# Two recurrence units go from four accumulators to seven products, one attention unit goes the other way, and the first load, the last weights and the last sums are rearranged

## The chip, the core and the metric

The kernel runs on one core of a Trainium2 chip. The number is the device time of one launch in microseconds (us). TensorE (PE) multiplies, VectorE (DVE) and ScalarE (ACT) work on elements, GpSimd (POOL) does some element work, and SyncE (SP) issues nearly all transfers from memory.

## The reference

A hybrid trunk of two layers on 544 frames: 512 frames of a new stream and 32 of a running one. D_MODEL is 2048.

```python
def rec_layer(...):                        # layer 0
    proj = rms_norm(x, g) @ w_in           # 2048 -> 2048 + 2048 + 1024 + 1024
    xa, ga, xb, gb = split(proj)
    xa_c = causal_conv(xa, ...)            # width 4
    r, i = sigmoid(blocks of xa_c @ w_r + b_r), sigmoid(blocks of xa_c @ w_i + b_i)
    ya = scan(h = a_t * h + u_t)           # a, u from r, i, lam, xa_c
    yb = pool_mix(xb)                      # trailing means, per-group map, scale
    return x + concat(ya * silu(ga), yb * silu(gb)) @ w_out      # 3072 -> 2048

def att_layer(...):                        # layer 1
    q, k, v, gt = split(rms_norm(x, g) @ w_in)                   # 2048 -> 4 x 2048
    o = sb_attend(q, k, v)                 # 16 heads, stick-breaking: a suffix sum over the keys
    return x + (o * silu(gt)) @ w_out      # 2048 -> 2048
# rms_norm(., norm_final) of the end; keys, values and states are outputs too
```

## The kernel before

Activations lie as 128 features by 544 frames, in two halves of 272 frames (H1, H2). A product in full precision is three TensorE products of split numbers: `mm3` gives high weight times high activation (line 108), high weight times low activation (L109) and low weight times high activation (L110), 128x272 each. Weights come by SP's queue into `wraw` (line 195, 384 KB in a tile of 128x768, seven buffers) and are split by `wsplit`: ACT copies the high part `wh` (L203), DVE subtracts it to get `wl` (L204), three buffers each. Activations are split the same way (`xh`, L230, and `xl`, L231).

A *unit* multiplies 2 x 128 output features by 2048 inputs. Twelve of the sixteen input blocks lie as a 2x2 square of blocks B11, B12, B21, B22 (six times 128 inputs by one half of the frames each), the other four lie in `XP`. There are two forms:

- `plain_unit`: four accumulators, 64 triples, so 192 matmuls. It splits four 128x768 weight tiles and the `XP` tiles, and DVE takes each accumulator out with one multiplication (`scaled_out`, L449).
- `unit`: seven products of six triples and 16 triples for `XP`, so 58 triples, 174 matmuls. For it DVE makes four sums of weight tiles (L385, L389, L394, L400, 128x768), splits seven weight tiles instead of four, adds four products up (L408) and adds an addend to each of the four results (L447). It also needs four blocks T1 to T4, sums of the activation blocks, built once for a layer by `sums_by_pairs`: `loads` fetches, `makes` adds (L283 to L285) and splits, `lastload` and `three` make T4 (L299).

Layer 0 has 16 recurrence units n = 0 to 15 (all plain before), eight pool units (`unit`) and the output projection (eight units). The gates of unit n (`back`, 12 matmuls into `pg`) are called at hook 2 of unit n+1. A hook is a function called between two parts of a unit, so that other work stands among the unit's own. Layer 1 has 16 heads h with two units each: `ha` (queries and keys) and `hb` (values and gate). Before, ha of head 0 is plain, with the three parts of the sums in its hooks 1, 2 and 3, and all others are `unit`s. Behind the output projection comes a *last part* for the four `XP` blocks: for each half of the frames and each of 16 output blocks m it takes a 128x512 weight tile, four triples, an add to `x3` (L1187), a square and a sum of squares (L1193). The final norm follows: `rstd_sums` gives the sums of squares to TensorE (L137), and `finish` scales (L1172) and stores. The first half's 16 `finish` calls stand in the second half's loop at m >= 8.

Code stands in the order in which it is called, but a scheduler orders each engine's instructions; `high_priority` moves what is in it ahead of other work that is ready.

## Time and profile before

| | |
|---|---|
| median of 3 runs | 1927.06 us (1926.83 to 1929.6) |
| the profiled execution | 1924.38 us, span 1922.6 us |
| granted TensorE clock, mean | 0.996 of full speed (2.4 GHz) |
| PE busy | 1890.3 us (98%) |
| DVE busy | 1526.8 us (79%) |
| ACT busy | 935.0 us (49%) |
| POOL busy | 181.8 us (9%) |

The span runs from the first to the last instruction; 1.78 us of the profiled time lie around it. Busy shares are means over all stages.

### The profile page before, as it was taken

How to read it: one execution, taken by the hardware profiler on the slowest of the kernel's cores; microseconds unless marked ns; L12 is line 12 of the kernel's file. 1: busy time of each engine (PE TensorE's matmuls, PEld its weight loads, DVE VectorE, ACT ScalarE, POOL GpSimd, SP SyncE). 2: the span in 40 equal slices, each digit the busy share in tenths (PEclk: the TensorE clock that was granted, in tenths of full speed). 3: DMA queues.
4: the chain of work that ended last, by engine and by line, in shares of the span. 5: the costliest groups of instructions: out<-in, count | busy, mean ns of one | idle time of the engine just before them, and what ended most of it. 6: DMA issues, size and time to landing. Idle time of an engine off the chain costs nothing.

```text
span 1922.6 us, 37274 instructions
## 1 busy us (share of the span) xinstructions
PE 1890.3 (98%) x14872; PEld 1871.7 (97%) x14872; DVE 1526.8 (79%) x2487; ACT 935.0 (49%) x1313; POOL 181.8 (9%) x294
## 2 busy tenths in 40 slices
PE   8999999999999999999999999999999999999997
PEld 8999999999999999999899999999999999999997
DVE  8766687689888666567988888888888888897987
ACT  7766666665335433335544444444444444454443
POOL 0000012011010000000211111111111101110000
PEclk9999999999999999999999999999999999999998
DMA  6454443323337645458333333334333433385344
GB/s 223 118 151 132 127 150 122 101 84 117 106 108 240 205 142 165 138 157 247 109 97 104 120 101 110 104 117 128 92 106 117 120 94 106 106 273 177 124 128 150
DMA packets 133215, 260.37 MB, mean 135 GB/s; under 512 B 16113, under 2 KB 44017, under 8 KB 133041
## 3 DMA queue, kind: packets, MB, share of 16 engines
q1 hardware_dynamic: 131808, 256.59, 43.2%
q8 instruction: 117, 1.92, 0.4%
q10 hardware_dynamic: 1152, 1.11, 0.2%
q14 instruction: 58, 0.47, 0.1%
q0 software_dynamic: 80, 0.28, 0.0%
HBM read 220.98 MB, written 36.95 MB: 134 GB/s over the span
## 4 chain that ended last, share of the span: by engine, by line
PE 79%; DVE 12%; DMA 4%; issue 3%; ACT 1%; POOL 0%; SPq 0%; DVEq 0%; ACTq 0%; POOLq 0%
PE pp L108 24%; PE pp L110 24%; PE pp L109 24%; DVE wl L204 4%; DMA wraw<-in_w_in_att 2%; DVE big L907 1%; PE pm L109 1%; DMA T<-x2g 1%; PE pm L110 1%; PE pa L924 1%; PE pm L108 1%; PE pg L108 1%; DVE xl L231 1%; PE pg L109 1%; DMA wraw<-in_w_in_rec 1%
## 5 line engine op out<-in xcount | busy, mean ns | idle before, releaser
L108 PE MATMUL pp<-xh,wh 128*128 128x272 f32 x3156 | 912.7, 289 | 11.3 <-ACT wh L203 7.5
L110 PE MATMUL pp<-xh,wl 128*128 128x272 f32 x3156 | 909.3, 288 | 3.2 <-DVE wl L204 3.0
L109 PE MATMUL pp<-xl,wh 128*128 128x272 f32 x3156 | 907.0, 288 | 0.1
L203 ACT ACTIVATE wh<-wraw 128x768 fp32r<-128x768 f32 (+2 forms) x634 | 494.9, 783 | 771.5 <-PE pp L109 526.5
L204 DVE TENSOR_TENSOR wl<-wraw,wh 128x768 fp32r<-128x768 f32 (+2 forms) x634 | 553.9, 878 | 148.8 <-ACT wh L203 145.2
L108 PEld LDWEIGHTS pp<-xh,wh 128*128 128x128 f32 x3156 | 595.2, 189 | 13.6 <-ACT wh L203 8.1
L110 PEld LDWEIGHTS pp<-xh,wl 128*128 128x128 f32 x3156 | 593.9, 188 | 6.7 <-DVE wl L204 6.3
L109 PEld LDWEIGHTS pp<-xl,wh 128*128 128x128 f32 x3156 | 594.5, 188 | 0.8 <-DVE xl L231 0.3
L110 PE MATMUL pp<-xp,wl 128*128 128x272 f32 x1152 | 331.6, 288 | 0.0
L108 PE MATMUL pp<-xp,wh 128*128 128x272 f32 x1152 | 331.4, 288 | 0.0
L109 PE MATMUL pp<-xp,wh 128*128 128x272 f32 x1152 | 330.0, 286 | 0.0
L108 PEld LDWEIGHTS pp<-xp,wh 128*128 128x128 f32 x1152 | 217.3, 189 | 1.1 <-issue 1.1
L110 PEld LDWEIGHTS pp<-xp,wl 128*128 128x128 f32 x1152 | 216.6, 188 | 0.0
L109 PEld LDWEIGHTS pp<-xp,wh 128*128 128x128 f32 x1152 | 216.2, 188 | 0.0
L447 DVE TENSOR_TENSOR e<-pp,e 128x272 f32<-128x272 f32 x156 | 65.5, 438 | 42.2 <-PE pp L110 38.3
L408 DVE TENSOR_TENSOR e<-pp,e 128x272 f32<-128x272 f32 x200 | 82.0, 430 | 5.4 <-PE pp L110 4.7
L109 PE MATMUL pp<-T,wh 128*128 128x272 f32 x256 | 73.7, 288 | 0.0
L108 PE MATMUL pp<-T,wh 128*128 128x272 f32 x256 | 73.7, 288 | 0.0
L110 PE MATMUL pp<-T,wl 128*128 128x272 f32 x256 | 73.5, 287 | 0.0
L230 ACT ACTIVATE xh<-T 128x544 fp32r<-128x544 f32 x72 | 46.4, 655 | 47.7 <-DVE T L283 14.4
L385 DVE TENSOR_TENSOR wraw<-wraw,wraw 128x768 f32<-128x768 f32 x50 | 47.6, 952 | 22.6 <-DMA wraw<-in_w_in_att 8.1
L209 ACT ACTIVATE T<-T 128x544 fp32r<-128x544 f32 (+1 forms) x72 | 45.1, 645 | 35.9 <-DMA T<-in_cv 15.6
(254 smaller groups left out, 2115.4 us busy)
## 6 DMA issues: line engine op xcount, KB each, us to landing
wraw<-in_w_in_att SPq DMA_DIRECT2D x128, 384.0 KB, 3.3
wraw<-in_w_in_rec SPq DMA_DIRECT2D x96, 384.0 KB, 3.3
wraw<-in_w_out_rec SPq DMA_DIRECT2D x64, 384.0 KB, 3.6
wraw<-in_w_in_att SPq DMA_DIRECT2D x64, 256.0 KB, 3.2
wraw<-in_w_in_rec SPq DMA_DIRECT2D x48, 256.0 KB, 3.2
wraw<-in_w_out_att SPq DMA_DIRECT2D x32, 384.0 KB, 3.8
...
```

Of the source, the lines that this page charges most:

```text
L108: nc.tensor.matmul(out, wh, xh, start=start, stop=False)
L109: nc.tensor.matmul(out, wh, xl, start=False, stop=False)
L110: nc.tensor.matmul(out, wl, xh, start=False, stop=stop)
L203: nc.scalar.activation(hi, src, AF.Copy)
L204: nc.vector.tensor_tensor(lo, src, f(hi), ALU.subtract)
L209: nc.scalar.activation(a, src, AF.Copy)
L230: nc.scalar.activation(h, src, AF.Copy)
L231: nc.vector.tensor_tensor(l, src, f(h), ALU.subtract)
L385: nc.vector.tensor_tensor(w[1], w[0], w[1], ALU.subtract)
L408: nc.vector.tensor_tensor(sm[name], acc[p], sm[other], ALU.add)
L447: nc.vector.tensor_tensor(src, bk, addend, ALU.add)
L907: nc.vector.tensor_tensor_scan(inc[:, o:o + w][:, ::-1], s, s, 1.0, ALU.mult, ALU.min)
```

## The change

1. **Start.** The first weight tile comes in two transfers, 128x128 and 128x640, and is split in two.
2. **Recurrence.** The sums T1 to T4 of this layer are made over units 10 to 13 (loads at hook 4 of 10, 11, 12, makes at hook 0 of 11, 12, 13, T4 at hook 0 of 14), and units 14 and 15 become `unit`s.
3. **Attention.** hb of head 0 becomes plain; the sums' parts go to hb of head 0 (hooks 0 and 1) and ha of head 1 (hook 0).
4. **Last part.** The first half keeps its 16 split weight tiles in the space of the activation blocks, and the second half uses them again. The add to `x3` is given high priority, the first half's 16 `finish` calls are spread over m = 4 to 13, and its reciprocal roots come earlier (m = 1 and 3, before 2 and 6).

```diff
-    def wsplit(src):
+    def wsplit(src, cut=0):
...
-        nc.scalar.activation(hi, src, AF.Copy)
-        nc.vector.tensor_tensor(lo, src, f(hi), ALU.subtract)
+        for a, b in ((0, cut), (cut, n)):
+            if a < b:
+                nc.scalar.activation(hi[:, a:b, :], src[:, a:b, :], AF.Copy)
+                nc.vector.tensor_tensor(lo[:, a:b, :], src[:, a:b, :], f(hi[:, a:b, :]), ALU.subtract)
...
-        def chunk(m, c):
-            early.append(raw(w_in_rec[m, :, c * NS:min((c + 1) * NS, KT)]))
+        def chunk(m, c, cut=0):
+
+            src = w_in_rec[m, :, c * NS:min((c + 1) * NS, KT)]
+            if cut:
+                t = raw()
+                nc.sync.dma_start(t[:, :cut * P], flat(src[:, :cut]))
+                nc.sync.dma_start(t[:, cut * P:], flat(src[:, cut:]))
+            else:
+                t = raw(src)
+            early.append((t, cut))
...
-        chunk(0, 0)
+        chunk(0, 0, 1)
...
-        one, two, three = sums(xgd)
+        loads, makes, lastload, three = sums_by_pairs(xgd)
...
-            if n == 9:
-                with_hooks(hk, {4: [one]})
-            if n == 10:
-                with_hooks(hk, {4: [two]})
-            if n == NRB - 1:
-                with_hooks(hk, {3: [three]})
-            plain_unit(srcs[n], rg_out(c), hk)
+            if 10 <= n <= 12:
+                with_hooks(hk, {4: [loads[n - 10]]})
+            if 11 <= n <= 13:
+                with_hooks(hk, {0: [makes[n - 11]]})
+            if n == 13:
+                with_hooks(hk, {4: [lastload]})
+            if n == 14:
+                with_hooks(hk, {0: [three]})
+            (plain_unit if n < 14 else unit)(srcs[n], rg_out(c), hk)
...
                 with_hooks(ha, {0: [lambda: pend.append(rows(x2g))],
-                                1: [lambda: box.append(rstd_sums(rps, 0, N)), one, lambda: pend.pop()()],
-                                2: [two], 3: [three],
+                                1: [lambda: box.append(rstd_sums(rps, 0, N)), lambda: pend.pop()()],
                                 4: [spread_rbc]})
+                with_hooks(hb, {0: [one], 1: [two]})
...
+            if h == 1:
+                with_hooks(ha, {0: [three]})
...
-            unit((w_in_att[4 * h + 2], w_in_att[4 * h + 3]), att_out(c), hb, LAST if h == NH - 1 else ORDER)
+            if h:
+                unit((w_in_att[4 * h + 2], w_in_att[4 * h + 3]), att_out(c), hb, LAST if h == NH - 1 else ORDER)
+            else:
+                plain_unit((w_in_att[2], w_in_att[3]), att_out(c), hb)
...
+        def last_weights(m):
+            if m == len(kept):
+                if m % 3 == 0:
+                    sl = SLOT[ORDER[m // 3]]
+                    room[:] = [xs.tile([P, 3, 4, P], F32R, tag=f"{q}{sl}", name=nm("wlast")) for q in ("xh", "xl")]
+                with tc.high_priority():
+                    src = raw(w_out_att[m, :, 2 * NS:]).rearrange("p (a b) -> p a b", b=P)
+                    hi, lo = (r[:, m % 3] for r in room)
+                    nc.scalar.activation(hi, src, AF.Copy)
+                    nc.vector.tensor_tensor(lo, src, f(hi), ALU.subtract)
+                kept.append((hi, lo))
+            return kept[m]
...
-                if hf == 1 and m == 2:
+                if hf == 1 and m == 1:
...
-                if hf == 1 and m == 6:
-                    nc.scalar.activation(rbc[:, H1], rstd_spread(rps, rst), AF.Copy)
-                with tc.high_priority():
-                    hi, lo = wsplit(raw(w_out_att[m, :, 2 * NS:]))
+                if hf == 1 and m == 3:
+                    with tc.high_priority():
+                        nc.scalar.activation(rbc[:, H1], rstd_spread(rps, rst), AF.Copy)
+                hi, lo = last_weights(m)
...
-                nc.vector.tensor_tensor(x3[m][:, s], x3[m][:, s], ps, ALU.add)
+                with tc.high_priority():
+                    nc.vector.tensor_tensor(x3[m][:, s], x3[m][:, s], ps, ALU.add)
...
-                if hf == 1 and m >= 8:
-                    finish(2 * (m - 8), 0, rbc[:, H1])
-                    finish(2 * (m - 8) + 1, 0, rbc[:, H1])
+                if hf == 1 and 4 <= m < 14:
+                    for q in range(16 * (m - 4) // 10, 16 * (m - 3) // 10):
+                        finish(q, 0, rbc[:, H1])
```

Three places in the order of DVE's instructions. A line of after stands 2 lines later in the code than in before from line 204 on, later by more further down (L285 of after is L283 of before, L449 is L447, L451 is L449, L1221 is L1187, L1189 is L1172). The first place is where T4 is made (its subtractions write `T_`). Before, in plain unit 11 (the call stands in unit 15, the scheduler takes it as soon as its operands are there), with two weight splits (`wl`) among them:

```order
L299 TENSOR_TENSOR T_3549<-T_3549,xh_443_3518 128x544
L204 TENSOR_TENSOR wl_3767<-wraw_3764,wh_3766 128x768
L588 TENSOR_TENSOR big_3629<-ev_3622,big_3629 128x548
L299 TENSOR_TENSOR T_3549<-T_3549,xl_444_3519 128x544
L299 TENSOR_TENSOR T_3551<-T_3551,xh_443_3518 128x544
L299 TENSOR_TENSOR T_3553<-T_3553,xh_443_3518 128x544
L299 TENSOR_TENSOR T_3551<-T_3551,xl_444_3519 128x544
L299 TENSOR_TENSOR T_3553<-T_3553,xl_444_3519 128x544
L204 TENSOR_TENSOR wl_3809<-wraw_3806,wh_3808 128x768
```

After, in unit 14, which has become a `unit`:

```order
L206 TENSOR_TENSOR wl_4690<-wraw_4687,wh_4689 128x768
L301 TENSOR_TENSOR T_4434<-T_4434,xl_451_3591 128x544
L402 TENSOR_TENSOR wraw_4687<-wraw_4687,wraw_4563 128x768
L387 TENSOR_TENSOR wraw_4847<-wraw_4845,wraw_4847 128x768
L410 TENSOR_TENSOR e_4683<-pp_4664,e_4657 128x272
L410 TENSOR_TENSOR e_4588<-pp_4664,e_4588 128x272
L233 TENSOR_TENSOR xl_565_4518<-T_4434,xh_564_4517 128x544
L301 TENSOR_TENSOR T_4436<-T_4436,xh_450_3590 128x544
L206 TENSOR_TENSOR wl_4714<-wraw_4687,wh_4713 128x768
L206 TENSOR_TENSOR wl_4739<-wraw_4736,wh_4738 128x512
L391 TENSOR_TENSOR wraw_4877<-wraw_4849,wraw_4847 128x768
L206 TENSOR_TENSOR wl_4774<-wraw_4535,wh_4773 128x768
```

T4's subtractions (L299, now L301) and their splits (L233) stand now among weight sums (L402, L387, L391) and additions of products (L410) of the unit itself.

The second place is the first head of the attention. Before, where ha of head 0 ends, its accumulators `pp` are taken out into `T_` (L449) behind the sums of the activation blocks (L283 to L285) and their splits (`xl`, L231):

```order
L283 TENSOR_TENSOR T_10940<-T_10940,T_10936 128x544
L231 TENSOR_TENSOR xl_1543_11009<-T_10932,xh_1542_11008 128x544
L284 TENSOR_TENSOR T_10936<-T_10936,T_10938 128x544
L231 TENSOR_TENSOR xl_1545_11011<-T_10940,xh_1544_11010 128x544
L285 TENSOR_TENSOR T_10938<-T_10940,T_10938 128x544
L204 TENSOR_TENSOR wl_11234<-wraw_11226,wh_11233 128x768
L231 TENSOR_TENSOR xl_1543_11009<-T_10938,xh_1542_11008 128x544
L394 TENSOR_TENSOR wraw_11226<-wraw_11226,wraw_11259 128x768
L449 TENSOR_TENSOR T_11179<-pp_10859,rbc 128x272
L449 TENSOR_TENSOR T_11179<-pp_10860,rbc 128x272
L204 TENSOR_TENSOR wl_11262<-wraw_11259,wh_11261 128x768
L231 TENSOR_TENSOR xl_1541_11007<-T_10936,xh_1540_11006 128x544
```

After, at the same end of ha of head 0:

```order
L451 TENSOR_TENSOR T_11151<-pp_10902,rbc 128x272
L451 TENSOR_TENSOR T_11151<-pp_10903,rbc 128x272
L206 TENSOR_TENSOR wl_11305<-wraw_11302,wh_11304 128x768
L387 TENSOR_TENSOR wraw_11546<-wraw_11544,wraw_11546 128x768
L451 TENSOR_TENSOR T_11184<-pp_10904,rbc 128x272
L451 TENSOR_TENSOR T_11184<-pp_10905,rbc 128x272
L212 TENSOR_TENSOR T_11188<-T_11151,T_11187 128x544
L206 TENSOR_TENSOR wl_11347<-wraw_11344,wh_11346 128x768
L212 TENSOR_TENSOR T_11194<-T_11184,T_11193 128x544
L391 TENSOR_TENSOR wraw_11601<-wraw_11548,wraw_11546 128x768
L206 TENSOR_TENSOR wl_11420<-wraw_11417,wh_11419 128x768
L285 TENSOR_TENSOR T_11206<-T_11206,T_11202 128x544
```

The taking out (L451) now comes ahead of the first sum (L285), which stands in hb; one weight sum (L387) and one more (L391) of ha of head 1 stand between them.

The third place is the end of the last part's second half. Before, behind the last additions to `x3` (L1187), with `finish` multiplications (L1172) among them:

```order
L1187 TENSOR_TENSOR big_22480<-big_22480,pp_23509 128x272
L1172 SCALAR_TENSOR_TENSOR T_22093<-T_22093,vec,rbc 128x272
L1172 SCALAR_TENSOR_TENSOR T_22094<-T_22094,vec,rbc 128x272
L1193 TENSOR_TENSOR sqacc<-sqacc,e_23529 128x272
L1187 TENSOR_TENSOR big_22480<-big_22480,pp_23536 128x272
L1172 SCALAR_TENSOR_TENSOR big_22287<-big_22287,vec,rbc 128x272 x2
L1193 TENSOR_TENSOR sqacc<-sqacc,e_23556 128x272
L1187 TENSOR_TENSOR big_22681<-big_22681,pp_23563 128x272
L1172 SCALAR_TENSOR_TENSOR big_22480<-big_22480,vec,rbc 128x272 x2
L1187 TENSOR_TENSOR big_22681<-big_22681,pp_23589 128x272
L1172 SCALAR_TENSOR_TENSOR big_22681<-big_22681,vec,rbc 128x272 x2
L148 TENSOR_SCALAR rs_71<-pa_23615 128x3
```

After:

```order
L1221 TENSOR_TENSOR big_22310<-big_22310,pp_23408 128x272
L1189 SCALAR_TENSOR_TENSOR big_22704<-big_22704,vec,rbc 128x272 x2
L1221 TENSOR_TENSOR big_22310<-big_22310,pp_23429 128x272
L1227 TENSOR_TENSOR sqacc<-sqacc,e_23422 128x272
L1227 TENSOR_TENSOR sqacc<-sqacc,e_23443 128x272
L1221 TENSOR_TENSOR big_22503<-big_22503,pp_23448 128x272
L1227 TENSOR_TENSOR sqacc<-sqacc,e_23462 128x272
L1221 TENSOR_TENSOR big_22503<-big_22503,pp_23469 128x272
L1227 TENSOR_TENSOR sqacc<-sqacc,e_23483 128x272
L1221 TENSOR_TENSOR big_22704<-big_22704,pp_23490 128x272
L1221 TENSOR_TENSOR big_22704<-big_22704,pp_23506 128x272
L148 TENSOR_SCALAR rs_71<-pa_23522 128x3
```

The `finish` multiplications (L1189 now) are gone from the last six additions (L1221).

## Rows read from the trace of the kernel before

**Rows 1.** The page: the span, and busy time, share of the span and instructions of each engine.

```profile
span 1922.6 us, 37274 instructions
...
PE 1890.3 (98%) x14872; PEld 1871.7 (97%) x14872; DVE 1526.8 (79%) x2487; ACT 935.0 (49%) x1313; POOL 181.8 (9%) x294
```

**Rows 2.** Busy time by stretch, in one of the recurrence's last units (343.00 on), its very last (394.20 on) and the first three pool units: the stretch in us, its length, then PE, PEld, DVE, ACT and POOL busy (instructions in it), clock, DMA share, GB/s.

```profile
343.00:368.60 25.60, 25.60 (x206) 25.60 (x206) 16.44 (x27) 15.61 (x20) 1.87 (x5) 1.00 0.32 99
...
394.20:419.80 25.60, 25.60 (x207) 25.60 (x206) 19.12 (x30) 16.96 (x23) 2.41 (x4) 1.00 0.24 74
419.80:443.00 23.20, 23.07 (x180) 22.51 (x180) 22.03 (x37) 16.43 (x22) 3.62 (x7) 1.00 0.39 117
443.00:466.00 23.00, 22.32 (x178) 22.01 (x177) 22.64 (x44) 11.07 (x15) 3.13 (x5) 1.00 0.39 116
466.00:489.00 23.00, 23.00 (x187) 23.00 (x186) 19.28 (x32) 8.62 (x12) 1.25 (x2) 1.00 0.37 117
```

**Rows 3.** DVE's groups with shapes from 419.8 to 443 us, where the first pool unit (a `unit`) runs: busy us, mean ns.

```profile
L204 DVE TENSOR_TENSOR wl<-wraw,wh 128x768 fp32r<-128x768 f32 x6 | 5.7, 950 | 0.1
...
L408 DVE TENSOR_TENSOR e<-pp,e 128x272 f32<-128x272 f32 x4 | 1.6, 425 | 0.0
...
L385 DVE TENSOR_TENSOR wraw<-wraw,wraw 128x768 f32<-128x768 f32 x1 | 0.9, 939 | 0.0
L447 DVE TENSOR_TENSOR e<-pp,e 128x272 f32<-128x272 f32 x2 | 0.9, 432 | 0.0
```

**Rows 4.** DVE's groups with shapes from 905 to 962 us, where the attention's sums are made.

```profile
L231 DVE TENSOR_TENSOR xl<-T,xh 128x544 fp32r<-128x544 f32 x12 | 8.6, 716 | 0.0
...
L299 DVE TENSOR_TENSOR T<-T,xl 128x544 f32<-128x544 f32 x3 | 2.1, 713 | 0.0
```

**Rows 5.** Timelines of DVE and of PE in the plain unit around 364 us: the split of the low part of a weight tile, and the first matmul of the next unit's first tile that reads such a part (start, length).

```profile
363.83 0.95 DVE L204 TENSOR_TENSOR wl<-wraw,wh 128x768 fp32r<-128x768 f32 x1
...
368.88 0.29 PE L110 MATMUL pp<-xh,wl 128*128 128x272 f32 x1
```

**Rows 6.** PE's waits from 395 to 470 us (total, times, longest).

```profile
PE pg L108 <- ACT T L209: 0.7, 1, 0.7
```

**Rows 7.** Busy time by stretch around the attention's first units, columns as in rows 2.

```profile
888.00:905.50 17.50, 17.50 (x145) 17.50 (x144) 10.98 (x24) 8.09 (x12) 4.15 (x12) 1.00 0.69 201
905.50:930.00 24.50, 21.53 (x168) 20.90 (x168) 24.47 (x39) 13.84 (x21) 8.38 (x2) 1.00 0.56 176
930.00:962.00 32.00, 30.78 (x239) 29.77 (x238) 29.52 (x47) 15.28 (x20) 4.98 (x7) 1.00 0.33 104
```

**Rows 8.** PE's waits from 880 to 965 us.

```profile
PE pp L108 <- ACT xh L230: 1.4, 1, 1.4
PE pp L108 <- DVE T L449: 1.2, 1, 1.2
PE pp L110 <- DVE wl L204: 1.0, 1, 1.0
PE pp L108 <- ACT wh L203: 0.4, 1, 0.4
```

**Rows 9.** PE's timeline behind one of these waits: two matmuls with ten steps between them (start, length).

```profile
915.84 0.28 PE L109 MATMUL pp<-xl,wh 128*128 128x272 f32 x1
...
917.09 0.28 PE L110 MATMUL pp<-xh,wl 128*128 128x272 f32 x1
```

**Rows 10.** DVE's timeline where the attention's sums begin.

```profile
905.49 0.73 DVE L283 TENSOR_TENSOR T<-T,T 128x544 f32<-128x544 f32 x1 [0.90 <-DMA T<-x2g]
```

**Rows 11.** ACT's timeline in the first 12 us.

```profile
4.38 0.52 ACT L496 ACTIVATE xh<-xraw,vec 128x272 fp32r<-128x272 f32 x1 [0.93 <-DMA xraw<-in_xT]
...
7.77 4.24 ACT L496 ACTIVATE xh<-xraw,vec 128x272 fp32r<-128x272 f32 x10 [0.28 <-DMA xraw<-in_xT]
```

**Rows 12.** Transfers issued in the first 10 us: count, KB of one, median us from issue to landing.

```profile
vec<-in_vecs SPq DMA_DIRECT2D x1, 92.0 KB, 2.0
```

**Rows 13.** The chain of waits in the first 9 us: start, length, what.

```profile
1.25 0.42 SPq L483
...
1.72 4.50 DMA wraw<-in_w_in_rec
...
7.13 0.59 PE pp L108
```

**Rows 14.** Busy time by stretch after the start, columns as in rows 2.

```profile
9.00:11.00 2.00, 2.00 (x10) 2.00 (x10) 2.00 (x6) 2.00 (x6) 0.00 (x0) 1.00 1.05 411
```

**Rows 15.** PE's timeline at the end: the last matmul of the last part, and the first sums of squares behind it.

```profile
1903.46 0.29 PE L110 MATMUL pp<-xp,wl 128*128 128x272 f32 x1
1905.91 0.80 PE L137 MATMUL pa<-ones,sqacc 128*128 128x2 f32 x6 [2.16 <-DVE sqacc L1193]
```

**Rows 16.** DVE's and ACT's timelines at the same end: two `finish` in one row, the last add to `x3`, and the last square.

```profile
1904.51 0.90 DVE L1172 SCALAR_TENSOR_TENSOR big<-big,vec,rbc 128x272 f32<-128x272 f32 x2
...
1906.87 0.42 DVE L1187 TENSOR_TENSOR big<-big,pp 128x272 f32<-128x272 f32 x1
...
1907.32 0.43 ACT L1196 ACTIVATE T<-big 128x272 f32<-128x272 f32 x1 [0.74 <-DVE big L1187]
```

**Rows 17.** The same add and square in the first half, where no `finish` stands.

```profile
1877.20 0.44 DVE L1187 TENSOR_TENSOR big<-big,pp 128x272 f32<-128x272 f32 x1 [0.23 <-PE pp L110]
...
1877.67 0.43 ACT L1196 ACTIVATE T<-big 128x272 f32<-128x272 f32 x1
```

7 lines of the change are left out of this document (4 added, 3 removed).

## The prediction, on record before the changed kernel was run

> **What bounds the kernel now.** I read the page first: PE is busy for 1890.3 of 1922.6 us [rows 1]. So the time is the number of matmuls times their distance, and what PE waits besides. The distance comes from PE's timeline: ten steps from 915.84 to 917.09 us, 0.125 us each [rows 9]. What changes the number of matmuls changes the time by that, unless another engine then holds PE up.
>
> The second view is the busy time by stretch [rows 2]. A late plain unit takes 25.6 us (192 matmuls and 12 for gates, 204 x 0.125 = 25.5), and DVE works for 16.44 us of it. In the pool units, which are already in seven products, DVE works for 22.03 of 23.2 and 22.64 of 23.0 us: there it is nearly the bound, and PE already loses something. From 419.8 to 466 us it issues 180 + 178 = 358 matmuls, 44.75 us of work in 46.2, so 1.45 us are lost; 0.7 of it is one wait for a gate's operand [rows 6].
>
> The third place is the start of the attention. From 905.5 to 930 us DVE is busy for 24.47 of 24.50 us, then for 29.52 of 32 [rows 7], and four waits of PE stand there, 4.0 us together [rows 8]. By the count it is 407 matmuls in 56.5 us, 50.9 of work, so 5.6 lost; some of the counted are narrower ones, so the loss could be a little more. I take 5.1, a choice near the middle of 4.0 and 5.6. The sums of the activation blocks begin at 905.49 us, after a wait for their transfer [rows 10].
>
> The fourth place is the end. The last matmul of the last part starts at 1903.46 us, the sums of squares behind it at 1905.91 [rows 15], because DVE still has `finish` work: the last add to x3 starts at 1906.87 and the square behind it ends at 1907.75 [rows 16].
>
> **The recurrence's units 14 and 15.** Each loses 18 matmuls: 2 x 18 x 0.125 = 4.5 us less on PE. Each gains on DVE three more splits (3 x 0.950), four weight sums (4 x 0.939), four additions of products (4 x 0.425) and four addends (4 x 0.432) [rows 3], together 10.0 us. T4 is now made in unit 14: six subtractions (0.713) and three splits (0.716) [rows 4], 6.4 us. So unit 14 needs 16.44 + 10.0 + 6.4 = 32.9 us of DVE, unit 15 needs 19.12 [rows 2] less the three T4 splits that before stood there (2.15), plus 10.0, which is 27.0. PE needs 174 + 12 = 186 matmuls, 23.25 us for each. DVE is short by 9.65 + 3.75 = 13.4 us. That is the heart of this change: the stage goes over from PE to DVE for two units.
>
> What absorbs it? Ahead of it, the low part of a weight tile was ready at 364.78 and first read at 368.88 us [rows 5], a lead of 4.1 us that can be eaten. Unit 13 has room to build that lead: one block of sums costs there 3 x 0.713 + 3 x 0.716 = 4.3 us (the additions priced by the nearest one of the same shape), 20.7 of 25.5 us in all. Behind it, the pool units have 1.2, 0.4 and 3.7 us of room [rows 2], and the gate work of unit 15 may slide that far, so I give 3.7, the largest, since the first two already hold waits. 13.4 - 4.1 - 3.7 = 5.6 us of waits stay, in the place of the 1.45 there now. The part gives -4.5 + 5.6 - 1.45 = about -0.3. Bounds: nothing more waits than now, -4.5; the whole shortage shows, -4.5 + 13.4 - 1.45 = +7.5. Units 10 to 13, where the rest of the sums are made one block at a time, have 9 us of room each (25.6 - 16.44); a block of 4.3 costs nothing there. If the room were gone, it would be 4.3 for each of three.
>
> The Trainium skill ("TensorE: Matmul & The Clock Gate", section Back-to-back issue gap) gives the distance of isolated matmuls at the full clock as columns through 2.4 GHz and 2.5 ns, 115.8 ns for 272 columns; the 125 ns of the row are 8% more. By the page the net 18 matmuls that leave the kernel would be worth 2.1 us, by the row 2.25, so the row is used.
>
> **The attention's first head.** hb of head 0 becomes plain: 18 more matmuls, +2.25 us. In turn DVE gets 10.0 us less there, and two of the four waits lose their reason: the accumulators of ha are now taken out ahead of the sums (the wait of 1.2 for L449), and hb doesn't read joined blocks any more (the 1.4 for xh) [rows 8]. But the sums themselves (19 us on DVE: three blocks of 4.3 and T4's 6.4) don't get cheaper. They move into hb, where DVE also runs the first head's scans, and ha of head 1 can't begin its joined products before they are done. From 905.5 to 962 us DVE then has 24.47 + 29.52 - 10.0 = 44.0 us of work against 50.9 + 2.25 = 53.1 of PE: no longer full, but lumpy. For the waits that stay I have two bounds: 1.45, as where the first pool unit joins, and 5.1, as now. I take the middle, 3.3. The part gives 2.25 - 5.1 + 3.3 = about +0.45; bounds -1.4 and +2.25.
>
> **The start.** Now the first weight tile of 384 KB lands 4.50 us after its issue at 1.72, and the first matmul starts at 7.13 [rows 13]; the first row of x is split from 4.38 on [rows 11]. A piece of 64 KB isn't in the trace: the smallest transfer here, 92 KB, took 2.0 us [rows 12], the full tile 4.5, so it lands between 3.7 and 6.2. Nearest is the first. Then the first matmul could start near 5.3 us, 1.8 earlier. But the second input block needs the next row of x, whose split starts at 7.77 [rows 11], and from 9 to 11 us ACT and DVE are busy without a pause [rows 14]: they set the pace, not PE's start. Only the first block's matmuls that now run behind the row's arrival, about two, come earlier; ten are counted in the 2.0 us of [rows 14], so 0.2 us each, 0.4 together. Bounds: -1.8 (all of it), and +0.4, if one more transfer ahead of the rows makes them late by its issue (0.42 us of SP's queue [rows 13]). I take -0.4.
>
> **The end.** In the first half, where no `finish` stands, the last add begins right as the matmul ends, 1877.20, and the square ends at 1878.10 [rows 17], 0.90 later. The second half's last matmul ends at 1903.75, so its square could end at 1904.65 instead of 1907.75: 3.1 us. Six adds at the end are free of `finish` now, but a sum of squares may still stand ahead of the last add, 0.4 us. So -2.7; bounds -3.1 and 0 (the tail behind is bound by something else).
>
> **At nothing.** Half the last weights' transfers and splits are gone: PE's triples cover both now, with no wait listed there. The new tiles go into space that the last projection unit still reads, so a split may start late in the first half; one is at most 0.95 us of DVE. x3's priority costs the `finish` behind it nothing, since they are off the path until the end.
>
> **The sum.** -0.3 + 0.45 - 0.4 - 2.7 = -2.95 us. The profiled execution (1922.6 span, 1924.38 with what lies around it) would be 1921.4; the median shown is 2.7 higher, so 1927.06 - 2.95 = 1924.1. About 0.2% (3.85 us) is what a measurement of this kernel can tell from no change: the forecast lies inside it.
>
> **Rivals.**
> - *DVE's shortage is hidden.* If the scheduler makes unit 14's weight sums well ahead and lets gate work slide over several pool units, the waits stay at 1.45: the recurrence gives -4.5, the sum is -7.15, 1919.9 us. For it speaks the room in units 10 to 13; against it that only three split tiles can be held, so work can't be made far ahead. 0.17.
> - *The attention's start runs free.* Waits fall to 1.45, the part gives -1.4, the sum -4.8, 1922.3. For it: 44 us of DVE work in 53. Against: the sums' transfers still can't start before the projection's last rows exist, and T4 stands directly ahead of head 1. 0.20.
> - *Slower: DVE becomes the bound from unit 14 to the second pool unit.* Nothing absorbs the 13.4 us, because T4's nine instructions stand among weight sums that the next product needs, and splits come late one by one. The part gives +7.5, the sum +4.85, 1931.9. It decides once PE's waits between 365 and 470 us pass 4.5 + 1.45 + 2.65 = 8.6 us. 0.10.
> - *The end's gain does not come.* The last transfers or the roots bind anyway: -0.25, 1926.8. Against it speaks the wait of 2.16 us that PE shows there [rows 15]. 0.10.
> - My forecast: 0.43.
>
> **Chances.** Faster by over 0.2%: the first two rivals, 0.37, and 0.06 of the forecast's own spread; 0.43. Slower: 0.10 and 0.01. Within: 0.46. The range goes from 1918.5, which takes in the hidden shortage with a little more at the start, to 1928.5, which leaves out most of the slower case. The forecast's own range is 1921.5 to 1926.5.
>
> **What would show it.** In the changed trace: 18 matmuls fewer on PE. DVE over 95% busy in units 14 and 15, and PE waits of 4 to 7 us together from there to the second pool unit, on wl, pp additions or a gate operand; below 2 the first rival holds, above 8.6 the third. At the attention the waits on L449's line and on joined xh are gone from head 0, and new ones stand at head 1's first unit; 3.3 us together. First matmul near 5.3 us, with a pause before the second input block. At the end the last add within 0.7 us of the last matmul. Wrong would be a part whose gain or loss differs from its term by more than 2 us, most likely the recurrence's, since its term is the difference of large numbers.

## The result: 6 us slower

Timed seven times beside the kernel before, the changed kernel has a median of 1933.84 us (1931.91 to 1936.63), the kernel before 1927.8 us. The ratio is 1.0031, with a 95% interval from 1.0022 to 1.0040: slower by about 6.0 us, outside the predicted range. The slow rival, DVE as the bound from unit 14 to the second pool unit, had given 1931.9.

The page of the changed kernel, as [rows 1] of before:

```profile
span 1932.4 us, 37185 instructions
PE 1892.9 (98%) x14854; PEld 1870.4 (97%) x14854; DVE 1527.3 (79%) x2487; ACT 928.1 (48%) x1302; POOL 185.1 (10%) x294
```

PE has 18 instructions fewer than before, as counted, and the span is 9.8 us longer. The profiled execution of before (1924.38) was a quick one of its kernel, so spans overstate the loss; below, traces are compared stage by stage and times by their ratios.

The busy time by stretch in the recurrence, which answers to [rows 2]: unit 13, units 14 and 15 (two lines), unit 15's end with the first pool unit, and two pool stretches. The columns are length, then busy us and instructions of PE, PEld, DVE, ACT and POOL, the granted clock, DMA share and GB/s.

```profile
343.00:366.00 23.00, 23.00 (x186) 23.00 (x185) 17.98 (x29) 16.02 (x22) 8.95 (x4) 1.00 0.49 141
366.00:391.00 25.00, 23.55 (x182) 22.71 (x181) 24.83 (x42) 17.04 (x24) 4.11 (x4) 1.00 0.35 109
391.00:415.00 24.00, 22.47 (x171) 21.37 (x170) 23.67 (x40) 12.82 (x18) 6.38 (x4) 1.00 0.23 70
415.00:440.00 25.00, 23.73 (x171) 22.92 (x171) 24.32 (x41) 17.50 (x24) 2.05 (x5) 0.93 0.37 113
440.00:464.00 24.00, 24.00 (x195) 24.00 (x194) 22.86 (x39) 15.02 (x20) 3.31 (x6) 1.00 0.38 111
464.00:488.00 24.00, 22.91 (x181) 22.48 (x181) 22.60 (x43) 11.15 (x15) 0.75 (x3) 1.00 0.37 115
435.10:439.10 4.00, 4.00 (x20) 4.00 (x21) 3.92 (x6) 0.65 (x1) 0.84 (x3) 0.57 0.34 98
```

From 366 to 440 us DVE works 72.82 of 74 us. In unit 13 just ahead, DVE works only 17.98 of 23 us, so 5 us of room go unused one unit too early. The last line is a stretch in which the granted clock is 0.57: its 20 matmuls stand about 0.2 us apart in place of 0.125 and cost some 1.6 us more.

PE's waits, after, from 365 to 470 us (what waited, for whom; us in total, times, the longest), beside [rows 6]:

```profile
PE pp L110 <- DVE wl L206: 4.4, 5, 1.4
PE pp L108 <- ACT wh L205: 0.6, 2, 0.3
PE pg L108 <- ACT big L597: 0.3, 1, 0.3
```

The list leaves small waits out. PE's matmuls in the same 105 us give the whole, before and after:

```profile
365.00:470.00 105.00, 104.19 (x826) 103.31 (x825) 87.09 (x147) 62.75 (x84) 12.15 (x22) 1.00 0.32 98
365.00:470.00 105.00, 99.65 (x757) 96.68 (x756) 102.60 (x173) 66.66 (x90) 16.59 (x22) 0.98 0.34 104
```

At 0.125 us each, 826 matmuls are 103.25 us of work, so 1.75 were lost before; 757 are 94.6, so 10.4 are lost after, 1.6 of them by the lower clock.

PE's waits from 880 to 965 us, after, beside [rows 8]:

```profile
PE pa L936 <- DVE big L920: 1.8, 1, 1.8
PE pp L108 <- DVE T L451: 0.8, 1, 0.8
```

Of the listed waits those from 365 to 470 us are new: before had 0.7 us there. From 880 to 965 us, 2.6 us remain of 4.0.

### The profile page after: what moved, and what is told of

The parts are those of the page before. It is cut to its first block, busy times and chain, and to the rows that moved or that the text cites. A ratio compares the mean times of both kernels' runs of the same rounds, so it can differ in the third digit from the quotient of the medians.

```text
span 1932.4 us, 37185 instructions
## 1 busy us (share of the span) xinstructions
PE 1892.9 (98%) x14854; PEld 1870.4 (97%) x14854; DVE 1527.3 (79%) x2487; ACT 928.1 (48%) x1302; POOL 185.1 (10%) x294
## 4 chain that ended last, share of the span: by engine, by line
PE 56%; DVE 10%; DMA 4%; issue 3%; ACT 0%; POOL 0%; DVEq 0%; SPq 0%; POOLq 0%; ACTq 0%
PE pp L110 17%; PE pp L108 17%; PE pp L109 17%; DVE wl L206 3%; DMA wraw<-in_w_in_att 2%; DVE big L919 1%; PE pm L109 1%; DMA wraw<-in_w_out_att 1%; PE pm L110 1%; PE pm L108 1%; PE pa L936 1%; DVE e L449 1%; DVE e L410 1%; PE pa L109 1%; PE pa L108 1%
## 5 line engine op out<-in xcount | busy, mean ns | idle before, releaser
L108 PE MATMUL pp<-xh,wh 128*128 128x272 f32 x3150 | 912.3, 290 | 10.8 <-ACT xh L498 7.0
L205 ACT ACTIVATE wh<-wraw 128x768 fp32r<-128x768 f32 (+3 forms) x606 | 476.6, 790 | 762.6 <-PE pp L109 514.6
L206 DVE TENSOR_TENSOR wl<-wraw,wh 128x768 fp32r<-128x768 f32 (+3 forms) x606 | 535.8, 888 | 141.9 <-ACT wh L205 139.9
L110 PE MATMUL pp<-xp,wl 128*128 128x272 f32 x1024 | 294.9, 288 | 1.5 <-DVE wl L206 1.5
L108 PE MATMUL pp<-xp,wh 128*128 128x272 f32 x1024 | 294.7, 288 | 0.0
L109 PE MATMUL pp<-xp,wh 128*128 128x272 f32 x1024 | 293.4, 287 | 0.0
L108 PEld LDWEIGHTS pp<-xp,wh 128*128 128x128 f32 x1024 | 193.4, 189 | 1.8 <-issue 1.1
L110 PEld LDWEIGHTS pp<-xp,wl 128*128 128x128 f32 x1024 | 192.7, 188 | 2.0 <-DVE wl L206 2.0
L109 PEld LDWEIGHTS pp<-xp,wh 128*128 128x128 f32 x1024 | 192.3, 188 | 0.0
L449 DVE TENSOR_TENSOR e<-pp,e 128x272 f32<-128x272 f32 x160 | 67.3, 439 | 40.5 <-PE pp L110 36.5
L410 DVE TENSOR_TENSOR e<-pp,e 128x272 f32<-128x272 f32 x204 | 83.9, 431 | 7.1 <-PE pp L110 6.1
L387 DVE TENSOR_TENSOR wraw<-wraw,wraw 128x768 f32<-128x768 f32 x51 | 49.1, 962 | 25.2 <-DMA wraw<-in_w_in_att 12.3
L391 DVE TENSOR_TENSOR wraw<-wraw,wraw 128x768 f32<-128x768 f32 x51 | 51.2, 1004 | 17.0 <-DMA wraw<-in_w_in_att 7.4
```

What stands on the lines that cost most here:

```text
L108: nc.tensor.matmul(out, wh, xh, start=start, stop=False)
L109: nc.tensor.matmul(out, wh, xl, start=False, stop=False)
L110: nc.tensor.matmul(out, wl, xh, start=False, stop=stop)
L205: nc.scalar.activation(hi[:, a:b, :], src[:, a:b, :], AF.Copy)
L206: nc.vector.tensor_tensor(lo[:, a:b, :], src[:, a:b, :], f(hi[:, a:b, :]), ALU.subtract)
L387: nc.vector.tensor_tensor(w[1], w[0], w[1], ALU.subtract)
```

## The experiments

All ratios are to the kernel before, timed in the same session; us are the ratio's difference from 1, times some 1929 us.

| kernel | ratio, 95% interval | us |
|---|---|---|
| part 1 alone (e1_start) | 1.0001 [0.9993, 1.0010] | +0.2 |
| part 2 alone (e2_rec) | 1.0028 [1.0019, 1.0038] | +5.4 |
| part 3 alone (e3_att) | 1.0000 [0.9991, 1.0008] | 0.0 |
| part 4 alone (e4_end) | 0.9987 [0.9978, 0.9995] | -2.5 |
| parts 2 and 3 (e18_rec_att) | 1.0046 [1.0031, 1.0061] | +8.9 |
| parts 1, 3 and 4 (e17_no_rec) | 0.9984 [0.9975, 0.9993] | -3.1 |

### One part at a time

The start alone:

```diff
-        chunk(0, 0)
+        chunk(0, 0, 1)
```


> Only the start is changed: the first weight tile in two transfers and two splits. In the trace of the changed kernel the first matmul starts 2.1 us earlier (5.00 us), but from the first scan on everything stands 0.5 us later. Theory A, the start only moves the wait: +0.5 us (0 to +1), with a PE pause of some 2 us before the second input block. Rival, the 0.5 came from elsewhere in that execution: the forecast's -0.4 us. A difference of this size is within what five rounds can just tell.

The recurrence alone:

```diff
-        one, two, three = sums(xgd)
+        loads, makes, lastload, three = sums_by_pairs(xgd)
...
-            plain_unit(srcs[n], rg_out(c), hk)
+            (plain_unit if n < 14 else unit)(srcs[n], rg_out(c), hk)
```


> Only the recurrence is changed: sums spread over units 10 to 13, units 14 and 15 in seven products. Theory A, DVE is the bound from unit 14 to the second pool unit and almost nothing absorbs its shortage of 13.4 us: the trace of the changed kernel stands 4.6 us later at the layer's output projection than after the start, so +4 to +5.5 us, with PE waits of about 10 us together between 365 and 470 us. Rival, the loss came with the other parts: the forecast's -0.3 us (-1.5 to +1).

The attention alone:

```diff
+                with_hooks(hb, {0: [one], 1: [two]})
...
+                plain_unit((w_in_att[2], w_in_att[3]), att_out(c), hb)
```


> Only the attention's first heads are changed: hb of head 0 plain, the sums' parts one unit later. In the changed kernel's trace the scan of head 1 stands 0.6 us earlier relative to the projection before it, and then 5.6 us are lost over heads 1 to 8, though DVE's and PE's order of instructions is the same there as before. Theory A, these later losses hang on this part (the shift of the first heads is carried on by waits for weight tiles): +3 to +5 us. Rival, they belong to that one execution or to another part: -1 to +0.5 us, with the offset against before constant from head 2 on.

The last part alone:

```diff
-                    hi, lo = wsplit(raw(w_out_att[m, :, 2 * NS:]))
+                hi, lo = last_weights(m)
...
+                with tc.high_priority():
+                    nc.vector.tensor_tensor(x3[m][:, s], x3[m][:, s], ps, ALU.add)
```


> Only the last part is changed: split weights kept for the second half, high priority for the add, finish spread, roots earlier. Theory A, the add no longer waits for finish: the time from the last matmul to the end falls by 4 us, and the new splits among the last projection unit cost up to 1 us: -3 to -4 us. Rival, the kept tiles wait for the space of the activation blocks and give the gain back in the first half: -1 to +1 us.

Start and attention are worth nothing that can be told, the last part gains 2.5 us, and the recurrence loses 5.4: the loss is in part 2. The four add up to +3.1 us, the whole change measures +6.0; the 2.9 us between are taken up further down. (Each of the five ratios has an interval of nearly 2 us to either side, so this difference of theirs is uncertain by some 4.)

PE's waits in e2_rec from 365 to 470 us:

```profile
PE pp L110 <- DVE wl L204: 4.9, 6, 1.4
PE pp L108 <- ACT wh L203: 0.6, 2, 0.3
```

These are the two largest lines, and the picture is that of the whole change. For a price by stage I take where the same matmul starts in two traces, from unit 13 to the last pool unit. The kernels whose recurrence is that of before lose 0.25 to 0.7 us there against the profiled execution of before, 0.42 on average; e2_rec loses 3.84, the whole change 4.04. Net of 0.42 that is 3.4 and 3.6 us. With the 4.5 us of matmuls that left, e2_rec has 7.9 us of new waits, where DVE was counted 13.4 us short. The other 2 us of its +5.4 lie outside this stage: in its profiled execution, the slowest of ten, the attention's start loses them and more (the wait of 3.50 us in the last section).

### Which of DVE's work shows

The edits of this section are shown against e2_rec. First, the sums over units 10 to 13 with plain units throughout, and with unit 15 alone in seven products:

```diff
-            (plain_unit if n < 14 else unit)(srcs[n], rg_out(c), hk)
+            plain_unit(srcs[n], rg_out(c), hk)
```


> The recurrence's sums spread over units 10 to 13 with T4 at the start of unit 14, as in the changed kernel, but units 14 and 15 stay plain (192 matmuls). Theory A, the loss comes from the shortage of DVE in seven products: without them unit 14 has 16.4 + 6.4 of 25.5 us, nothing waits, 0 us (-0.5 to +1). Rival, the spread sums or T4's place cost by themselves: +2 us or more, with waits on xl or wl in units 10 to 14.

```diff
-            (plain_unit if n < 14 else unit)(srcs[n], rg_out(c), hk)
+            (plain_unit if n < 15 else unit)(srcs[n], rg_out(c), hk)
```


> As the recurrence's part alone, but only unit 15 in seven products; T4 stands in unit 14, which is plain. 18 matmuls less, -2.25 us. Theory A, the shortage of DVE sets the loss: T4's 6.4 us fit into unit 14 (22.8 of 25.5 us), unit 15 is short by 3.75 us, so -2.25 + 2 to 3.75 = -0.3 to +1.5 us. Rival, each unit in seven products costs its full price whatever stands beside it (half of the +5.4 measured for two): +2.7 us.

And all sums, T4 among them, one unit earlier:

```diff
+            if 9 <= n <= 11:
+                with_hooks(hk, {4: [loads[n - 9]]})
...
-            if n == 14:
+            if n == 13:
                 with_hooks(hk, {0: [three]})
```


> As the recurrence's part alone, two units in seven products, but all sums one unit earlier: blocks in units 10 to 12, T4 in unit 13, which had 5 us of DVE to spare. 36 matmuls less, -4.5 us. Theory A, total DVE work in units 14 and 15 is what counts: the shortage falls by T4's 6.4 us to about 7, the waits from about 10 us to about 4, so -2 to 0 us against before (5.5 to 7 us better than the part as it was changed). Rival, the waits come from the order within a seven-product unit beside the recurrence's own chain, not from T4: +3 to +5.5 us, hardly better.

They came out at 1.0032 [1.0019, 1.0044], 1.0056 [1.0044, 1.0069] and 1.0041 [1.0028, 1.0055]: +6.2, +10.8 and +7.9 us. None answers its question, because each makes T4 while a plain unit has still to read block B12, whose space T4 takes; that unit multiplies T4's blocks in place of B12's, and its products wait for T4's split. PE's waits in e5_spread, 365 to 470 us:

```profile
PE pp L108 <- ACT xh L230: 2.3, 1, 2.3
PE pp L108 <- ACT wh L203: 1.5, 1, 1.5
PE pp L110 <- DVE wl L204: 1.5, 2, 1.2
```

The first line is that wait. It shows a bound which the prediction hadn't seen: T4's blocks can't be written before the last plain unit has read B12. That binds its three splits, 2.15 us of DVE. Its six subtractions, 4.3 us, write tiles of their own, and before they ran in unit 11, 100 us ahead of the splits; a kernel with seven products that leaves them there was not tried. The next two kernels respect the bound: T4 late in unit 13 (hook 3; the other sums one unit earlier, as in e9_t4early), and unit 15 alone in seven products with T4 late in unit 14.

```diff
-            if n == 14:
-                with_hooks(hk, {0: [three]})
+            if n == 13:
+                with_hooks(hk, {3: [three]})
```


> As the recurrence's part alone (two units in seven products, +5.4 us measured), but sums one unit earlier and T4 at hook 3 of unit 13, the first place where no plain unit reads the block any more whose space T4 takes. Theory A, every microsecond of DVE that a seven-product unit lacks is a wait: T4's 6.4 us leave unit 14, but the shortage of the units themselves stays (3.7 us each), so 36 matmuls less (-4.5) and about 7.5 of waits in the place of 8.5 and more: +2 to +4 us. Rival, as in the forecast, lead and room absorb what is left: -2 to 0 us.

```diff
-                with_hooks(hk, {0: [three]})
-            (plain_unit if n < 14 else unit)(srcs[n], rg_out(c), hk)
+                with_hooks(hk, {3: [three]})
+            (plain_unit if n < 15 else unit)(srcs[n], rg_out(c), hk)
```


> Only unit 15 in seven products, T4 at hook 3 of unit 14, which stays plain and whose last read of that block is past. (In the earlier run with one unit, and in the two beside it, T4 stood where a plain unit still read the block, so these three computed with a wrong block, and PE waited 2.4 us for it; this one does not.) 18 matmuls less, -2.25 us. Theory A, the unit's own shortage of 3.75 us shows in full: +1 to +2.5 us. Rival, one unit's shortage fits into the lead of 4.1 us: -2.25 to -1 us.

Then the weight sums, left out (e13_lean) and made on POOL (e14_pool):

```diff
-                    nc.vector.tensor_tensor(w[1], w[0], w[1], ALU.subtract)
+                    if not lean:
+                        nc.vector.tensor_tensor(w[1], w[0], w[1], ALU.subtract)
```


> As the recurrence's part alone, but the four weight sums of units 14 and 15 are left out (their products use the unsummed tiles), 4 x 0.95 us of DVE less in each unit; matmuls, transfers and splits stay. Theory A, DVE's load sets the waits: 7.6 us less of DVE takes 6 to 7.6 us from them, -2 to 0 us against before, 5 to 7 better than with the sums. Rival, the waits come from the chain of steps inside the unit (split behind split, three buffers), not from DVE's total: +3 us or more.

```diff
-                    nc.vector.tensor_tensor(w[1], w[0], w[1], ALU.subtract)
+                    ws.tensor_tensor(w[1], w[0], w[1], ALU.subtract)
...
+                unit(srcs[n], rg_out(c), hk, ws=nc.gpsimd)
```


> As the recurrence's part alone, but the four weight sums of units 14 and 15 stand on POOL, which is busy for 2 to 6 us of 25 there. DVE's load falls as in the kernel without them. POOL's time for 128x768 is not in any trace here. Theory A, it takes some 2 us and stands early enough: -2 to +1 us against before. Rival, POOL is slow or holds DVE up, and the sums arrive late: +5 us or more, with PE or DVE waiting for wraw from POOL.

| kernel | DVE short by (counted as in the prediction) | PE's loss over the stage, net | new waits (loss + matmuls that left) | ratio, 95% interval | us |
|---|---|---|---|---|---|
| e2_rec | 13.4 | 3.4 | 7.9 | 1.0028 [1.0019, 1.0038] | +5.4 |
| e10_t4in13 | 13.4 - 6.4 = 7.0 | 1.7 | 6.2 | 1.0017 [1.0008, 1.0026] | +3.3 |
| e13_lean | 13.4 - 8 x 0.95 = 5.8 | 1.05 | 5.55 | 1.0020 [1.0008, 1.0032] | +3.9 |
| e11_u15 | 3.75 (unit 15 alone) | 2.06 | 2.06 + 2.25 = 4.3 | 1.0041 [1.0028, 1.0054] | +7.9 |

Without T4's work 6.2 of 7.0 us of DVE's shortage still stand as waits of PE, without the weight sums 5.55 of 5.8; in e11_u15 more waits stand there than the count has, perhaps since part of T4's late work is in them. From e10_t4in13 to e2_rec DVE gets 6.4 us more to do and PE waits only 1.7 more; from e13_lean to e2_rec it gets 7.6 us more, and PE waits only 2.35 more. So either piece, taken out alone, was largely hidden, and most of the waits stay when it is gone: the count of DVE's shortage doesn't set them. (By the ratios, too, e10_t4in13 and e13_lean are 2.1 and 1.5 us better than e2_rec, which their intervals can't tell from nothing.) The recorded rival of e13_lean, that the waits come from the chain of steps inside a seven-product unit and not from DVE's total, had said +3 us or more, and +3.9 was measured, where theory A had -2 to 0. DVE's busy time from 366 to 440 us in e10_t4in13, then in e13_lean (72.49 in e2_rec):

```profile
366.00:440.00 74.00, 70.70 (x535) 67.51 (x534) 69.48 (x114) 46.63 (x65) 7.91 (x15) 1.00 0.34 98
366.00:440.00 74.00, 70.83 (x549) 68.86 (x548) 70.11 (x120) 50.34 (x70) 9.54 (x15) 1.00 0.34 100
```

DVE is still 94 and 95% busy there, and some of its idle time is waits of its own (1.8 us for a product in e10_t4in13, 2.1 us for `wh` in e13_lean). So a load that is nearly full and the order within the unit can both be the cause, and these runs don't part them. None of the four gains anything: two seven-product units in this place save 4.5 us of matmuls and cost 5.5 or more. All four cost more as a whole than in this stage: e11_u15 loses 2.06 us here and 7.9 in all, e10_t4in13 1.7 and 3.3, e13_lean 1.05 and 3.9. In e11_u15's trace the rest lies in layer 1 and is taken up below; the profiled executions of e10_t4in13 and e13_lean (1930.08 and 1930.23 us, against medians of 1934.15 and 1933.08) were quick ones and don't show it. PE's waits, 365 to 470 us, in e10_t4in13 (the two largest lines), then e13_lean, then e11_u15:

```profile
PE pp L110 <- DVE wl L204: 2.5, 4, 1.0
PE pp L108 <- ACT wh L203: 1.4, 4, 0.4
```

```profile
PE pp L110 <- DVE wl L204: 2.9, 4, 1.1
PE pp L108 <- ACT wh L203: 0.9, 2, 0.6
```

```profile
PE pp L110 <- DVE wl L204: 1.9, 3, 0.8
PE pp L108 <- ACT wh L203: 1.0, 2, 0.6
```

In all three the product that waits longest is the one that reads `wl`: splits come late, whatever stands ahead of them on DVE. On POOL the sums made it worse, 1.0075 [1.0063, 1.0087], +14.5 us. Its waits, and POOL's sums from 360 to 440 us (operation and shape, count; busy us, mean ns; idle time before):

```profile
PE pp L110 <- DVE wl L204: 8.8, 6, 3.3
```

```profile
L394 POOL TENSOR_TENSOR wraw<-wraw,wraw 128x768 f32<-128x768 f32 x2 | 4.6, 2286 | 7.0 <-issue 7.0
L400 POOL TENSOR_TENSOR wraw<-wraw,wraw 128x768 f32<-128x768 f32 x2 | 4.1, 2051 | 4.0 <-DVE wl L204 4.0
```

One such sum takes 2.05 to 2.29 us in these rows against 0.94 on DVE [rows 3]; that the splits which read it come that much later, and PE's 8.8 us of waits from it, is a reading of these rows.

### The end: the order or the kept weights

The order of part 4 without the kept weights (the edit against e4_end), and the kept weights without the order (against the kernel before):

```diff
-                hi, lo = last_weights(m)
+                with tc.high_priority():
+                    hi, lo = wsplit(raw(w_out_att[m, :, 2 * NS:]))
```


> Of the last part only the order: high priority for the add, finish calls spread over m = 4 to 13, roots earlier; the second half loads and splits its weights again as before. Theory A, the gain of the whole part (-2.5 us measured) is that of the add no longer behind finish, and keeping the weights gives nothing: -2.5 to -4 us. Rival, without the kept weights DVE's splits (16 of 0.69 us) leave no room for the spread finish calls and the last add is late again: -1 to 0 us.

```diff
-                with tc.high_priority():
-                    hi, lo = wsplit(raw(w_out_att[m, :, 2 * NS:]))
+                hi, lo = last_weights(m)
```


> Of the last part only the kept weights: the second half neither loads nor splits, the order of adds and finish stays as before. The order alone measured +1.2 (0.0006) us, both together -2.5. Theory A, DVE's 16 splits are what crowds the second half, and without them the adds are on time anyway: -2 to -3 us. Rival, both are needed: -1 to +1 us, with the last add still behind finish calls.

e7_sums: 1.0006 [0.9997, 1.0015]; e8_keep: 0.9994 [0.9984, 1.0004]; both together had given 0.9987. PE's timeline at the end of e7_sums, of e8_keep and of e4_end (start, duration; in brackets the idle time ahead and what ended it):

```profile
1909.89 0.29 PE L110 MATMUL pp<-xp,wl 128*128 128x272 f32 x1
1913.91 0.80 PE L137 MATMUL pa<-ones,sqacc 128*128 128x2 f32 x6 [3.73 <-DVE sqacc L1211]
```

```profile
1912.59 0.29 PE L110 MATMUL pp<-xp,wlast 128*128 128x272 f32 x1
1912.71 0.72 PE L137 MATMUL pa<-ones,sqacc 128*128 128x2 f32 x6
```

```profile
1908.86 0.29 PE L110 MATMUL pp<-xp,wlast 128*128 128x272 f32 x1
1908.99 0.72 PE L137 MATMUL pa<-ones,sqacc 128*128 128x2 f32 x6
```

With the new order alone the wait is longer than before (3.73 against 2.16 us, [rows 15]), though the last add there starts as its product ends, at 1910.21 us: what comes late are the sums of squares behind it, the last at 1913.34 us, with five `finish` multiplications among them. With the kept weights alone it is gone, since DVE and ACT have no splits left in the second half; but that kernel loses some 2.6 us in the first half, where PE shows one wait of 1.4 us on DVE. So without the kept weights the order gains nothing. Whether they need the order is not told: e8_keep and e4_end lie 1.4 us apart, within their intervals.

### Why the whole is more than its parts

Two combinations, parts 2 and 3, and all but part 2:

```diff
-            plain_unit(srcs[n], rg_out(c), hk)
+            (plain_unit if n < 14 else unit)(srcs[n], rg_out(c), hk)
...
+                plain_unit((w_in_att[2], w_in_att[3]), att_out(c), hb)
```


> The recurrence's and the attention's part together, without start and end. If parts add up: 5.4 + 0.0 = +5.4 us (+4 to +7). If they interact, by the turn of the buffers or otherwise: +8 us or more.

```diff
-        chunk(0, 0)
+        chunk(0, 0, 1)
...
+                plain_unit((w_in_att[2], w_in_att[3]), att_out(c), hb)
...
+                hi, lo = last_weights(m)
```


> The whole change without the recurrence's part. If parts add up: 0.2 + 0.0 - 2.5 = -2.3 us (-4 to -1). If the start, the attention and the end interact: 0 us or more.

Parts 2 and 3 measure +8.9 us where their single times add to 5.4; without part 2 the rest measures -3.1 where its parts add to -2.3. So the surplus, if it is one (each difference is uncertain by 3 to 4 us), comes with part 2 in company of part 3. **e17_no_rec, the change without part 2, is faster than before** by 0.16% (0.07 to 0.25%), where the whole change is 0.31% slower; from part 4 alone (0.13%) it can't be told.

Where the surplus stands can be seen from the first transposition of each head's weights (the line with `wt[:, bk, cc:cc + P]`), as its start less that of the profiled execution of before:

| kernel | head 0 | head 1 | head 6 | head 15 |
|---|---|---|---|---|
| e1_start | 3.0 | 2.8 | 3.7 | 6.1 |
| e4_end | 2.1 | 1.9 | 2.6 | 4.0 |
| e17_no_rec | -10.7 | 2.6 | 3.4 | 3.9 |
| the whole change | -8.9 | 4.4 | 9.9 | 10.5 |
| e18_rec_att | -8.2 | 6.1 | 8.9 | 10.6 |
| e19_after_e2 | -8.9 | 4.7 | 7.3 | 9.4 |
| e2_rec | 10.7 | 10.6 | 11.8 | 13.7 |
| e11_u15 | 6.9 | 7.7 | 11.9 | 14.7 |

(Head 0 stands earlier wherever part 3 is in, since its sums lie behind it then.) From head 1 to head 6 the whole change loses 5.5 us, parts 2 and 3 lose 2.8 and e19_after_e2 (below) 2.6; e1_start, e4_end and e17_no_rec lose 0.7 to 0.9. PE's waits from 1000 to 1800 us, first of before, then after:

```profile
PE pm L914 <- DVE T L449: 1.1, 1, 1.1
PE pp L110 <- DVE wl L204: 0.7, 2, 0.4
```

```profile
PE pp L110 <- DVE wl L206: 4.0, 6, 1.0
PE pm L109 <- DVE big L940: 1.6, 1, 1.6
PE pm L926 <- DVE T L451: 1.1, 1, 1.1
```

The new ones are waits of about 1 us on `wl` in the heads, where the order of instructions on each engine is the same as before. Two causes were tried: that part 2 shifts the turn in which buffers are handed out, first that of the weight tiles, then that of the tiles `e`. The kernel before with one more, respectively three more, dummy tiles in the output projection of the first layer:

```diff
+                nc.gpsimd.memset(raw()[:, :2], 0.0)
```


> The kernel before with one weight buffer taken and hardly used (a small fill by POOL) at unit 1 of layer 0's output projection: every weight tile behind it lies one buffer further on, and nothing else changes; each unit in seven products shifts this turn by one too. Theory T, the turn of the seven buffers matters for the attention's heads: +4 to +6 us, in 1.2 us waits at heads. Rival, the turn is of no account: -0.5 to +1 us.

```diff
+                for _ in range(3):
+                    nc.gpsimd.memset(e()[:, :2], 0.0)
```


> The kernel before with three e buffers taken and hardly used at unit 1 of layer 0's output projection, so that every later e tile lies three buffers further on; nothing else changes. Theory E, the turn of the five e buffers costs in the attention's heads: +4 to +6 us. Rival, where a tile lies is of no account and the surplus is carried in another way (or is scatter): -0.5 to +1 us.

And the whole change with two more of `e`, which brings back the turn of before:

```diff
+                for _ in range(2):
+                    nc.gpsimd.memset(e()[:, :2], 0.0)
```


> The changed kernel with two e buffers more taken at the same place, which brings their turn at the heads back to that of before. Theory E: the surplus of 3 us goes, +2 to +3.5 us against before. Rival: +6 us (+4.5 to +7.5), as the changed kernel.

0.9996 [0.9987, 1.0005], 1.0001 [0.9992, 1.0010] and 1.0030 [1.0019, 1.0041]: neither turn alone is the cause; both together were not tried. The last kernel still shows the waits on `wl` from 1000 to 1800 us:

```profile
PE pp L110 <- DVE wl L206: 3.6, 6, 1.0
```

What makes the heads lose 2 to 4 us more stays open. Part 2 alone doesn't do it: from head 1 to head 15 e2_rec loses 3.1 us, as e1_start does with 3.3. e11_u15, where only unit 15 of the recurrence is in seven products, loses 7.0 (the whole change 6.1), though it loses less in the recurrence. Each of these is one execution.

## Why the prediction was wrong

**The recurrence, -0.3 forecast, +3.6 measured.** The count of work held: 18 matmuls fewer in all, DVE 98% busy from 366 to 440 us. The step that failed is "What absorbs it?". It let 4.1 us of lead and 3.7 of room behind, 7.8 together, swallow the shortage beyond what the earlier waits of 1.45 stood for. 13.4 us short, the kernel has 3.6 + 4.5 = 8.1 us of new waits, where 5.6 - 1.45 = 4.15 were forecast; with the earlier 1.45 that is 9.55, so 13.4 - 9.55 = 3.85 us were absorbed where 7.8 were taken (4.05 in e2_rec). It looks as if the lead of 4.1 had served and the room of 3.7 had not, but no fixed amount comes off the shortage: counted alike, e10_t4in13 has 7.65 us of waits with 7.0 short, e13_lean 7.0 with 5.8. What the runs show in place of the step is that halving the shortage took away 1.7 to 2.35 us of waits and left 5.55 to 6.2. Why so much stays is open, as said above.

The lead of 4.1 was a poor term in two ways, as far as can be read. It was a difference read at one tile, not room that DVE has: unit 13 left 5 us of DVE idle just ahead and built no more. And the pool units behind are themselves 95 and 98% full [rows 2], so that whatever lead is eaten in unit 14 is missing there; that this is the reason is a reading of the busy rows, not tried. The room of 3.7, the largest of three, gave none: across that third pool unit the whole change falls back by 1.5 us more, read from the matmuls that start at 464 and 488 us before.

The rival that nothing is absorbed was at +7.5 for this part, the forecast at -0.3, the truth in the middle; its chance of 0.10 was too small for a term that is the difference of large numbers, as the prediction itself called it. Its mark, waits above 8.6 us between 365 and 470 us, is not passed by the listed waits (4.4 + 0.6 + 0.3 = 5.3), but by the count of matmuls, with which the prediction had counted its 1.45: 10.4 us are lost there, 8.8 without the lower clock, just above it. So the rival's sign came, at half of its price.

**The attention, +0.45 forecast, 0.0 alone.** Right in size: 2.6 us of waits where 3.3 were taken. From 905 to 930 us, where the two largest waits of [rows 8] stood (1.2 and 1.4; the one of 1.0 stood at 955 us, outside the stretch in which the prediction put all four), PE now waits for nothing above the list's bound. Both waits left stand in head 1's first unit, as forecast: 0.8 at its first product, at 946.52 us, for the taking out of hb's accumulators (T at L451), and 1.8 at 951.93 us, for the product behind head 0's scan (L920). Neither is a wait for T4's blocks. T4's nine instructions stand among DVE's work there, from 937.86 to 961.82 us, so a part of the delay may be theirs; the place was right, the reason is not shown.

**The start, -0.4 forecast, +0.2 measured (not told from zero).** The first matmul starts at 5.00 us, near the 5.3 forecast, and then pauses, to no gain. PE's timeline, ACT's and the transfers there:

```profile
5.00 0.60 PE L108 MATMUL pp<-xh,wh 128*128 128x272 f32 x1 [5.00 <-ACT xh L498]
...
8.32 1.14 PE L108 MATMUL pp<-xh,wh 128*128 128x272 f32 x2 [1.95 <-ACT xh L498]
```

```profile
4.23 0.31 ACT L205 ACTIVATE wh<-wraw 128x128 fp32r<-128x128 f32 x1 [0.76 <-DMA wraw<-in_w_in_rec]
...
7.12 0.74 ACT L205 ACTIVATE wh<-wraw 128x640 fp32r<-128x640 f32 x1 [2.16 <-DMA wraw<-in_w_in_rec]
7.76 4.35 ACT L498 ACTIVATE xh<-xraw,vec 128x272 fp32r<-128x272 f32 x10
```

```profile
wraw<-in_w_in_rec SPq DMA_DIRECT2D x1, 320.0 KB, 4.9
wraw<-in_w_in_rec SPq DMA_DIRECT2D x1, 64.0 KB, 2.5
```

The piece of 64 KB lands in 2.5 us, the rest of 320 KB in 4.9 (the whole had taken 4.50, [rows 13]), and the rows of x wait on ACT behind the rest's split. The prediction had the pause before the second input block; PE pauses already inside the first, for the second half (H2) of the first row. Before, that half was split ahead of the ten pieces of [rows 11]:

```profile
6.99 0.51 ACT L496 ACTIVATE xh<-xraw,vec 128x272 fp32r<-128x272 f32 x1
```

After, it is split at 7.76 us, and the next row, whose split stood at 7.77 before [rows 11], follows at 8.29 (at 7.96 in e1_start). So the early start is spent on the pause, and the rows that set the pace come 0.5 and 0.2 us later: by these traces the term had the wrong sign. The Trainium skill ("DMA: Bandwidth & Descriptors", section Anatomy of one DMA — SWDGE (gpsimd) path) gives some 2 us as the fixed cost of a transfer on GpSimd's path; these transfers go by SP's queue, and the row of 2.5 us for a fifth of the bytes, against 4.9, fits a fixed share of that size.

**The end, -2.7 forecast, -2.5 measured.** After, the last product and the sums of squares stand next to each other, and the last add follows its matmul, as foreseen:

```profile
1917.45 0.29 PE L110 MATMUL pp<-xp,wlast 128*128 128x272 f32 x1
1917.58 0.72 PE L137 MATMUL pa<-ones,sqacc 128*128 128x2 f32 x6
```

```profile
1917.78 0.44 DVE L1221 TENSOR_TENSOR big<-big,pp 128x272 f32<-128x272 f32 x1 [1.05 <-PE pp L110]
```

From the last product to the end of the span it is 1932.4 - 1917.45 = 14.95 us, 19.1 before: 4.2 gained, of which the first half and the last unit ahead give back about 1.2 (by part 4's trace). The size was right and the reason only half: the prediction put the gain on the adds' order and the kept weights "at nothing", while e7_sums shows that the order alone gives nothing.

**The surplus of 2.9 us**, if it is one, stood in no term: a part was thought to act only where its instructions are.
